# Layer 2's scan of a four-stage network: decay differences moved to ScalarE, trailing parts moved from GpSimd to VectorE

## The chip, the cores and the metric

The kernel runs on one core of a Trainium2 chip. The metric is the device time of one execution in microseconds, the median of several. The engines are named as the profile names them: PE is TensorE (matmuls), DVE is VectorE, ACT is ScalarE, POOL is GpSimd, SP is SyncE, which issues all of this kernel's transfers.

## The reference, cut to what matters

The network has two blocks, each over a sequence of 1024 positions with width 1024. The first block has two layers: one with a gated linear recurrence beside latent attention, and a state space layer, in which the change lies. The second block is a convolution and an attention side by side, an MLP and a gated projection. The state space layer computes, in chunks of 128 positions, with 32 heads of width 64 in 4 groups and a state of 128:

```
def _ssd_scan(x, dt, a_neg, bm, cm):
    ...
    cs = jnp.cumsum(a_dt, axis=2)
    cs_h = jnp.transpose(cs, (0, 1, 3, 4, 2))
    seg = cs_h[..., :, None] - cs_h[..., None, :]
    causal = jnp.tril(jnp.ones((L, L), dtype=bool))
    decay = jnp.where(causal, jnp.exp(jnp.where(causal, seg, 0.0)), 0.0)
    cb = jnp.einsum('bclgn,bcsgn->bcgls', cc, bc)
    y_diag = jnp.einsum('bcghls,bcsghp->bclghp', cb[:, :, :, None] * decay, xf)
    ...
    states = jnp.einsum('bclgn,bclghp->bcghpn', bc, xf * decay_states[..., None])
    ...
    y_off = jnp.einsum('bclgn,bcghpn->bclghp', cc, prev) * jnp.exp(cs)[..., None]
    return (y_diag + y_off).reshape(bsz, seqlen, n_heads, p_dim)
```

The output of the scan gets a skip term, is gated with silu(z), normalized by its group's mean square and projected back to width 1024. All of it is in float32.

## The kernel before

Every float32 product is made of three matmuls on halves: a number is split into a leading part (`hi`, a rounding to the matmul's format, cast on ACT) and a trailing part (`lo`, number minus `hi`, the helper `lo` on line 259), and `mm3` adds hi·hi, hi·lo and lo·hi (lines 188, 192, 193). So each operand of a matmul costs a cast on ACT and a subtraction, on DVE or POOL, whichever the caller names. `weights` (lines 168 to 184) does it for a weight: transfer to `wr`, cast to `wh` (line 179), subtraction to `wl`, in pieces of 128x512 with three buffers of each name; its subtraction goes to POOL unless the caller names an engine.

`phase_b` is the state space layer. It runs 32 steps: 8 units `u` (half a group, 4 heads) times 4 pairs of chunks `cpair`. A step has two halves. `stage1` transposes the inputs on PE, scales them by dt and by the decay to the chunk's end (`Xf`, line 896) and splits them (`Xh` on ACT, `Xl` on POOL). It loads the cumulated logs of the decay, broadcast over partitions, into `L` (128x1024; the tag L has one buffer), subtracts the column `cs_t` of each head and chunk and clips at zero (line 909, 8 instructions of 128x128 on DVE), takes the exponential (line 911, ACT), multiplies by the masked products `cbm` (line 914, DVE, two of 128x512), and splits the result (`Lh` line 916 on ACT, `Ll` on POOL). It also advances the state: a product, then `hs` (lines 932 and 933, DVE), split into `hh` (line 938, ACT) and `hl` (POOL). `stage2` multiplies state and decay matrices into the output: `et` (lines 969 to 986, DVE; line 974 adds the skip term), gates it (`zt`, line 989, DVE), squares it on ACT (line 995) and sums the squares into `acc2` on POOL (lines 997 and 1000). Between the steps, `project` makes the projections for later units (matrices of 128x1024 against all 1024 positions into the PSUM tile `g`): `proj_x` and `proj_bc` are followed by a convolution on DVE (lines 813 and 815), `proj_z` by a gate. At the end of a group `prep_bc` splits and multiplies the next group's B and C (`ch` on ACT, `cl` on POOL). In the last steps `part` starts the output projection, with inputs normalized by `y_act` (line 1072 on DVE, the cast on ACT, the subtraction on POOL). `finish_b` ends it.

The order on each engine is set by a scheduler, which places the instructions of the program by a simulated time line; each engine then works through its own list in order and waits where an instruction's inputs or buffers aren't ready.

Of the kernel before, what the change touches and what calls it, by code (L numbers as in the profile page):

```python
# [11 lines left out]
AF = mybir.ActivationFunctionType  # L12
A = mybir.AluOpType
# [36 lines left out]
class K:  # L50
    def __init__(self, ctx, tc, d):
        self.tc, self.nc, self.d = tc, tc.nc, d
        self.ctx = ctx
        nc = self.nc
        self.cp = ctx.enter_context(tc.tile_pool(name="cp", bufs=1))
        self.wp = ctx.enter_context(tc.tile_pool(name="wp", bufs=3))
        self.dp = ctx.enter_context(tc.tile_pool(name="dp", bufs=1, space=bass.MemoryType.DRAM))
        cp = self.cp
        self.vec = cp.tile([128, NVEC], F32, name="vec")
        self.XH = [cp.tile([128, T], F32R, name=f"XH{k}") for k in range(8)]  # L60
        self.XL = [cp.tile([128, T], F32R, name=f"XL{k}") for k in range(8)]
        self.uid = 0
        self.bp = ctx.enter_context(tc.tile_pool(name="bp", bufs=1, reuse_waits="tile"))
        self.pp = None
        self.it = self.iu = self.ib = 0
        self.side, self.pin = None, False

    @contextmanager
    def phase(self, ns, nh, nd=0, ne=0, nt=3, tmp_p=False):
# [98 lines left out]
    def weights(self, ap, kt, eng=None):  # L168

        nc = self.nc  # L170
        eng = eng or nc.gpsimd
        out = []
        for c in range(0, kt, 4):
            n = min(4, kt - c) * 128
            raw = self.wp.tile([128, HN], F32, tag="wr", bufs=3, name=self.nm("wr"))
            hi = self.wp.tile([128, HN], F32R, tag="wh", bufs=3, name=self.nm("wh"))
            lo = self.wp.tile([128, HN], F32R, tag="wl", bufs=3, name=self.nm("wl"))
            nc.sync.dma_start(raw[:, :n], ap[:, c * 128:c * 128 + n])
            nc.scalar.copy(hi[:, :n], raw[:, :n])  # L179
            self.lo(eng, lo[:, :n], raw[:, :n], hi[:, :n])  # L180
            for j in range(n // 128):
                out.append((hi[:, j * 128:j * 128 + 128], lo[:, j * 128:j * 128 + 128]))
        return out
# [564 lines left out]
    def phase_b(self):  # L748
        nc, v, P, R, cp, d = self.nc, self.v, self.P, self.R, self.cp, self.d
# [9 lines left out]


        first = self.first
        ps = first.pop(0)
        H = slice(0, 32)
        dt, e, cs = P("dt"), P("e"), P("cs")
# [23 lines left out]
        dt_t, w2_t, cs_t = tm[:, 0], tm[:, 1], tm[:, 2]  # L788
# [47 lines left out]
        def prep_bc(g):  # L836
# [10 lines left out]
            nc.scalar.copy(bh, b)  # L847
            self.lo(nc.vector, bl, b, bh)
            nc.scalar.copy(ch, cc)
            self.lo(nc.gpsimd, cl, cc, ch)  # L850
            cbm = P("cbm")
            for n in range(2):
                ps = self.t1()
# [24 lines left out]
        def stage1(u, cpair):  # L878
# [19 lines left out]
                                            fb[:, :, None].to_broadcast([128, 4, 64]), op=A.mult)  # L898
            Xh, Xl = R("Xh"), R("Xl")
            nc.scalar.copy(Xh, Xf)  # L900
            self.lo(nc.gpsimd, Xl, Xf, Xh)

            L = self.tag("L", "L")
            Lv = L.rearrange("p (c h l) -> p c h l", c=2, h=4)
# [1 line left out]
                              csd[c0:c0 + 2, h0:h0 + 4, :].rearrange("c h l -> c (h l)").partition_broadcast(128))  # L906
            for c in range(2):
                for h in range(4):
                    nc.vector.tensor_scalar(Lv[:, c, h, :], Lv[:, c, h, :], cs_t[:, (c0 + c) * 32 + h0 + h:(c0 + c) * 32 + h0 + h + 1],  # L909
                                            0.0, op0=A.subtract, op1=A.min)  # L910
            nc.scalar.activation(L, L, AF.Exp)
            cv = cbm.rearrange("p (c l) -> p c l", c=8)
            for c in range(2):
                nc.vector.tensor_tensor(Lv[:, c], Lv[:, c], cv[:, c0 + c:c0 + c + 1, :].to_broadcast([128, 4, 128]), op=A.mult)
            Lh, Ll = R("Lh"), R("Ll")
            nc.scalar.copy(Lh, L)
            self.lo(nc.gpsimd, Ll, L, Lh)

            prev = []
            pst = self.t1()  # L920
            for c in range(2):
# [14 lines left out]
                hh = self.ph.tile([128, 256], F32R, tag="hh", bufs=4, name=self.nm("hh"))  # L936
                hl = self.ph.tile([128, 256], F32R, tag="hl", bufs=4, name=self.nm("hl"))
                nc.scalar.copy(hh, hn)
                self.lo(nc.gpsimd, hl, hn, hh)
                hst[u] = hn, (hh, hl)  # L940
            stg[u, cpair] = Xh, Xl, Lh, Ll, prev

        def stage2(u, cpair):
# [50 lines left out]
            sq = et  # L994
            nc.scalar.activation(sq, zt, AF.Square)
            if hg == 0:
                nc.gpsimd.tensor_tensor(acc2[g][:, cols], sq[:, 0:256], sq[:, 256:], op=A.add)
            else:
                for p in range(2):
                    nc.gpsimd.tensor_tensor(acc2[g][:, cols], acc2[g][:, cols], sq[:, p * 256:p * 256 + 256], op=A.add)  # L1000
                if cpair % 2:
                    n = cpair // 2
                    s = slice(n * HN, n * HN + HN)
                    ps = self.u1()
                    nc.tensor.matmul(ps, self.ones, acc2[g][:, s], start=True, stop=True)
                    self.rstd_from(acc2[g][:, s], ps, 1.0 / 512, 1e-6)
                    nc.sync.dma_start(self.rsd[g:g + 1, s], acc2[g][0:1, s])
# [56 lines left out]
    def y_act(self, k, hi, lo):  # L1064

        nc, v = self.nc, self.v
        if k % 4 == 0:
            self.rs = self.P("rs")
            nc.sync.dma_start(self.rs, self.rsd[k // 4:k // 4 + 1, :].partition_broadcast(128))
        y = self.P("yl")  # L1070
        nc.sync.dma_start(y, self.yd[k * 128:k * 128 + 128, :])
        nc.vector.scalar_tensor_tensor(y, y, v("snorm", k), self.rs, op0=A.mult, op1=A.mult)
        nc.scalar.copy(hi, y)
        self.lo(nc.gpsimd, lo, y, hi)
        return self.prs(hi, lo)

    def finish_b(self):
        nc, v = self.nc, self.v
        act = [self.y_act(8 + k, self.R("yh"), self.R("yl")) for k in range(4)]
        t = [self.hs(self.P("t")) for m in range(8)]  # L1080
        for n in range(2):
# [844 lines left out]
```

## Time and profile before

| | |
|---|---|
| median of 3 runs | 2819.79 us (2819.03 to 2828.58) |
| profiled execution | 2823.64 us, span 2821.9 us |
| busy in the span: PE, DVE, ACT, POOL | 2639.9, 1998.7, 1366.2, 1091.5 us |
| instructions: PE, DVE, ACT, POOL | 12000, 2740, 2191, 737 |
| steps of the scan (first to last instruction of line 909) | from 576 to 1294 us |

The span is the time from the first to the last instruction of the profiled execution. An engine's busy time is the time in which it has at least one instruction running; instructions of an engine overlap a little at their ends, so a group's count times its mean is a little more than its busy time. A row of groups names the line, the engine, the operation, what is written and read, the shapes and the count; behind the bar stand the busy time, the mean duration and the idle time of the engine just ahead of such instructions.

### The profile page before, as it was taken

What the parts mean: (1) busy time and instruction counts of PE and PEld (TensorE: products, weight loads), DVE (VectorE), ACT (ScalarE), POOL (GpSimd) and SP (SyncE); (2) the same over time, 40 slices, a digit from 0 to 9 for tenths busy, and PEclk for the clock granted to TensorE, in tenths of its full rate; (3) what the DMA queues carried; (4) which work ended last, traced back from release to release, by engine and by line L of the source; (5) the groups of instructions that cost most, each with busy time, mean ns of one, the idle gap of its engine ahead of it and who ended that gap; (6) DMA issues with size and microseconds to landing.
All of it is one profiled execution on the core that took longest, in us unless ns stands there. A gap on an engine that the chain in (4) does not pass through costs nothing. (4 is left out here: it accounts for less than half of the span.)

```text
span 2821.9 us, 34684 instructions
## 1 busy us (share of the span) xinstructions
PE 2639.9 (94%) x12000; PEld 2104.9 (75%) x12000; DVE 1998.7 (71%) x2740; ACT 1366.2 (48%) x2191; POOL 1091.5 (39%) x737
## 2 busy tenths in 40 slices
PE   8999999998888999979899999999899999999997
PEld 6777887776677777758677777767677888887786
DVE  4774766779988899885487212889786666776676
ACT  5554755644443444433265313565665445343465
POOL 2633654445555555575555422656400000000024
PEclk9999999998999989989999999899999999999999
DMA  3444523443334334356533343544464445977324
GB/s 125 159 160 146 141 77 108 148 129 100 117 106 124 111 98 123 108 167 208 167 121 115 94 153 112 155 117 118 136 211 142 146 157 197 340 253 239 111 83 150
DMA packets 214420, 407.15 MB, mean 144 GB/s; under 512 B 22636, under 2 KB 61548, under 8 KB 214244
## 3 DMA queue, kind: packets, MB, share of 16 engines
q1 hardware_dynamic: 214244, 404.93, 44.7%
q8 instruction: 94, 1.54, 0.2%
q14 instruction: 82, 0.67, 0.1%
HBM read 297.35 MB, written 107.50 MB: 143 GB/s over the span
## 5 line engine op out<-in xcount | busy, mean ns | idle before, releaser
L259 POOL TENSOR_TENSOR wl<-wr,wh 128x512 fp32r<-128x512 f32 (+2 forms) x352 | 514.9, 1466 | 1247.3 <-ACT wh L179 1195.4
L188 PE MATMUL g<-XH,wh 128*128 128x512 f32 x1296 | 529.8, 409 | 12.5 <-ACT XH L354 7.5
L192 PE MATMUL g<-XL,wh 128*128 128x512 f32 x1296 | 527.8, 407 | 4.5 <-DVE XL L745 2.3
L193 PE MATMUL g<-XH,wl 128*128 128x512 f32 x1296 | 525.0, 405 | 3.4 <-POOL wl L259 3.4
L179 ACT CAST wh<-wr 128x512 fp32r<-128x512 f32 (+2 forms) x367 | 221.2, 603 | 395.8 <-PE g L192 153.6
L188 PEld LDWEIGHTS g<-XH,wh 128*128 128x128 f32 x1296 | 252.3, 195 | 74.6 <-ACT XH L354 8.2
L192 PEld LDWEIGHTS g<-XL,wh 128*128 128x128 f32 x1296 | 251.6, 194 | 66.4 <-issue 3.5
L193 PEld LDWEIGHTS g<-XH,wl 128*128 128x128 f32 x1296 | 251.7, 194 | 63.0 <-POOL wl L259 4.1
L192 PE MATMUL m<-XL,XH 128*128 128x512 f32 x368 | 145.1, 394 | 6.3 <-DVE XL L259 6.2
L188 PE MATMUL m<-XH,XH 128*128 128x512 f32 x368 | 143.7, 392 | 0.0
L193 PE MATMUL m<-XH,XL 128*128 128x512 f32 x368 | 143.6, 392 | 0.0
L188 PE MATMUL t<-XH,wh 128*128 128x512 f32 (+1 forms) x328 | 129.6, 395 | 4.8 <-ACT wh L179 4.8
L193 PE MATMUL t<-XH,wl 128*128 128x512 f32 (+1 forms) x328 | 130.5, 398 | 2.4 <-POOL wl L259 2.3
L192 PE MATMUL t<-XL,wh 128*128 128x512 f32 (+1 forms) x328 | 129.7, 396 | 0.0
L1281 POOL TENSOR_TENSOR sg<-sg,kp 128x639 f32<-128x639 f32 (+5 forms) x64 | 94.3, 1482 | 67.2 <-DVE kp L1280 60.3
L259 POOL TENSOR_TENSOR Xl<-Xf,Xh 128x1024 fp32r<-128x1024 f32 x32 | 87.0, 2718 | 74.8 <-ACT Xh L900 74.8
L1280 DVE TENSOR_TENSOR_SCAN kp<-kp,zero 128x640 f32<-128x640 f32 (+5 forms) x64 | 106.6, 1680 | 12.2 <-ACT kp L1276 10.8
L1612 ACT CAST XH<-a 128x1024 fp32r<-128x1024 f32 x46 | 48.1, 1049 | 137.5 <-PE m L192 109.9
L909 DVE TENSOR_SCALAR L<-L,tm 128x128 f32<-128x128 f32 x256 | 89.0, 415 | 22.7 <-DMA L<-csd 22.7
L259 DVE TENSOR_TENSOR wl<-wr,wh 128x512 fp32r<-128x512 f32 (+1 forms) x108 | 69.8, 668 | 48.7 <-ACT wh L1528 45.9
L813 DVE SCALAR_TENSOR_TENSOR xc<-xb,hw,xc 128x1021 f32<-128x1021 f32 (+2 forms) x63 | 102.0, 1621 | 3.0 <-ACT xc L810 2.5
L974 DVE SCALAR_TENSOR_TENSOR et<-xc,vec,et 128x256 f32<-128x256 f32 x64 | 102.3, 1637 | 0.4
(583 smaller groups left out, 6779.4 us busy)
## 6 DMA issues: line engine op xcount, KB each, us to landing
a<-w_down SPq DMA_DIRECT2D x64, 512.0 KB, 5.6
b<-hd SPq DMA_DIRECT2D x48, 512.0 KB, 5.7
wr<-wb_in SPq DMA_DIRECT2D x90, 256.0 KB, 3.2
wr<-wc_in SPq DMA_DIRECT2D x72, 256.0 KB, 2.9
L<-csd SPq DMA_DIRECT2D x32, 512.0 KB, 5.0
wr<-w_up SPq DMA_DIRECT2D x28, 512.0 KB, 3.7
wr<-wb_out SPq DMA_DIRECT2D x48, 256.0 KB, 4.5
hd<-t SPq DMA_DIRECT2D x48, 256.0 KB, 2.4
```

The source lines that it names most:

```text
L179: nc.scalar.copy(hi[:, :n], raw[:, :n])
L188: first = nc.tensor.matmul(ps, w[0], a[0], start=start, stop=False, skip_group_check=more)
L192: nc.tensor.matmul(ps, w[0], a[1], start=False, stop=False, skip_group_check=more)
L193: nc.tensor.matmul(ps, w[1], a[0], start=False, stop=stop, skip_group_check=more)
L259: eng.tensor_tensor(out, src, hi.bitcast(F32), op=A.subtract)
L813: nc.vector.scalar_tensor_tensor(xc[:, s:], xb[:, :T - s], hw[:, 24 * k + ci:24 * k + ci + 1], xc[:, s:], op0=A.mult, op1=A.add)
L909: nc.vector.tensor_scalar(Lv[:, c, h, :], Lv[:, c, h, :], cs_t[:, (c0 + c) * 32 + h0 + h:(c0 + c) * 32 + h0 + h + 1], 0.0, op0=A.subtract, ...
L974: nc.vector.scalar_tensor_tensor(ev[:, :, p, :], xt[p][:, cols].rearrange("p (c l) -> p c l", c=2), v("d_skip", 4 * g + 2 * hg + p), ev[:, ...
L1280: nc.vector.tensor_tensor_scan(rv, rv, zero.to_broadcast([128, W]), 1.0, op0=A.mult, op1=A.add)
L1281: nc.gpsimd.tensor_tensor(sg[:, :W - 1], sg[:, :W - 1], kp[:, 1:W], op=A.mult)
L1612: nc.scalar.copy(hi, x)
```

## The change

- The subtraction and the clip on `L` (8 instructions of 128x128 a step on DVE) become 8 activations on ACT, Relu of the column minus `L`; the exponential that follows gets the factor -1. The value is the same.
- The subtractions of `Xl`, `Ll`, `hl` and `cl`, and the sums of squares `acc2`, are put from POOL to DVE.
- In `phase_b` the trailing parts of weights (`wl`) and of `y_act` go to DVE; `finish_b` sets them back to POOL.

By count, 270 instructions go from POOL to DVE: 90 `wl` of 128x512; 32 `Xl`, 32 `Ll`, 4 `cl` and 8 `XL` of `y_act`, each 128x1024; 56 `hl` and 48 sums of 128x256. 256 instructions go from DVE to ACT. PE, SP and the loads of ACT's tables stay the same in number.

```
+        self.weng = tc.nc.gpsimd
...
-        eng = eng or nc.gpsimd
+        eng = eng or self.weng
...
+        self.weng = nc.vector
...
-            self.lo(nc.gpsimd, cl, cc, ch)
+            self.lo(nc.vector, cl, cc, ch)
...
-            self.lo(nc.gpsimd, Xl, Xf, Xh)
+            self.lo(nc.vector, Xl, Xf, Xh)
...
-                    nc.vector.tensor_scalar(Lv[:, c, h, :], Lv[:, c, h, :], cs_t[:, (c0 + c) * 32 + h0 + h:(c0 + c) * 32 + h0 + h + 1],
-                                            0.0, op0=A.subtract, op1=A.min)
-            nc.scalar.activation(L, L, AF.Exp)
+                    nc.scalar.activation(Lv[:, c, h, :], Lv[:, c, h, :], AF.Relu, scale=-1.0,
+                                         bias=cs_t[:, (c0 + c) * 32 + h0 + h:(c0 + c) * 32 + h0 + h + 1])
+            nc.scalar.activation(L, L, AF.Exp, scale=-1.0)
...
-            self.lo(nc.gpsimd, Ll, L, Lh)
+            self.lo(nc.vector, Ll, L, Lh)
...
-                self.lo(nc.gpsimd, hl, hn, hh)
+                self.lo(nc.vector, hl, hn, hh)
...
-                nc.gpsimd.tensor_tensor(acc2[g][:, cols], sq[:, 0:256], sq[:, 256:], op=A.add)
+                nc.vector.tensor_tensor(acc2[g][:, cols], sq[:, 0:256], sq[:, 256:], op=A.add)
...
-                    nc.gpsimd.tensor_tensor(acc2[g][:, cols], acc2[g][:, cols], sq[:, p * 256:p * 256 + 256], op=A.add)
+                    nc.vector.tensor_tensor(acc2[g][:, cols], acc2[g][:, cols], sq[:, p * 256:p * 256 + 256], op=A.add)
...
-        self.lo(nc.gpsimd, lo, y, hi)
+        self.lo(self.weng, lo, y, hi)
...
+        self.weng = nc.gpsimd
```

The scheduler orders the new program anew. One place shows how: the step whose decay matrix is `L_9064`, in the third group of heads. First DVE before, from that matrix's differences to the next step's inputs (in the changed file the lines of the scan are numbered two higher):

```order
L909 TENSOR_SCALAR L_9064<-L_9064,tm 128x128 x5
L932 TENSOR_TENSOR hs_8867<-hs_8858,dec 128x256
L909 TENSOR_SCALAR L_9064<-L_9064,tm 128x128 x3
L872 SCALAR_TENSOR_TENSOR z_8981<-z_8981,g_8932 128x1024
L914 TENSOR_TENSOR L_9064<-L_9064,cbm_8122 128x512 x2
L933 TENSOR_TENSOR hs_8867<-hs_8867,t_8854 128x256
L932 TENSOR_TENSOR hs_9085<-hs_8867,dec 128x256
L896 TENSOR_TENSOR Xf_9055<-t_9050,tm 128x256 x4
```

And DVE of the changed kernel around the same matrix:

```order
L260 TENSOR_TENSOR Xl_9061<-Xf_9055,Xh_9060 128x1024
L260 TENSOR_TENSOR wl_9328<-wr_9326,wh_9327 128x512
L260 TENSOR_TENSOR hl_8861<-hs_8858,hh_8860 128x256
L973 MEMSET et_9109 128x256
L916 TENSOR_TENSOR L_9064<-L_9064,cbm_8122 128x512 x2
L935 TENSOR_TENSOR hs_8867<-hs_8867,t_8854 128x256
L988 TENSOR_TENSOR et_8887<-et_8887,u_8906 64x256 x2
L934 TENSOR_TENSOR hs_9085<-hs_8867,dec 128x256
L991 SCALAR_TENSOR_TENSOR zt_8892<-et_8887,zt_8892 128x256 x2
L260 TENSOR_TENSOR Ll_9078<-L_9064,Lh_9077 128x1024
L935 TENSOR_TENSOR hs_9085<-hs_9085,t_9081 128x256
L260 TENSOR_TENSOR wl_9485<-wr_9483,wh_9484 128x512
```

The eight differences are gone from DVE's list, and the trailing parts stand in it between the other work, six rows (of this merged list) between the product of line 916 and the weight `wl_9485`.

ACT before, around the same matrix (line 911 is the exponential, 916 the cast of the product, 179 the cast of a weight):

```order
L938 CAST hh_8860<-hs_8858 128x256
L911 ACTIVATE L_9064<-L_9064 128x1024
L938 CAST hh_8870<-hs_8867 128x256
L179 CAST wh_9151<-wr_9150 128x512
L179 CAST wh_9321<-wr_9320 128x512
L871 ACTIVATE z_9046<-g_8997 128x1024
L900 CAST Xh_9060<-Xf_9055 128x1024
L916 CAST Lh_9077<-L_9064 128x1024
```

And ACT of the changed kernel (line 911 is now the difference, 913 the exponential, 918 the cast of the product, 180 the cast of a weight):

```order
L911 ACTIVATE L_9064<-L_9064,tm 128x128 x8
L902 CAST Xh_9060<-Xf_9055 128x1024
L180 CAST wh_9327<-wr_9326 128x512
L940 CAST hh_8860<-hs_8858 128x256
L913 ACTIVATE L_9064<-L_9064 128x1024
L918 CAST Lh_9077<-L_9064 128x1024
L180 CAST wh_9484<-wr_9483 128x512
L940 CAST hh_8870<-hs_8867 128x256
```

The eight differences stand in one block, and the casts `Xh_9060`, `wh_9327` and `hh_8860` stand behind that block.

## Rows read from the trace of the kernel before

**Rows 1.** Windows: us from start, length, busy of each engine (count), PEclk, DMA share.

```profile
core 0: us, PE busy (x) PEld busy (x) DVE busy (x) ACT busy (x) POOL busy (x), PEclk, DMA share, GB/s
576.00:1300.00 724.00, 641.36 (x3033) 520.69 (x3032) 625.73 (x966) 303.95 (x391) 408.73 (x255) 0.92 0.40 121
...
750.00:800.00 50.00, 47.54 (x244) 39.11 (x243) 39.46 (x65) 23.99 (x31) 27.29 (x19) 1.00 0.30 96
...
900.00:950.00 50.00, 43.87 (x216) 34.74 (x216) 48.17 (x66) 22.76 (x29) 27.69 (x17) 0.93 0.34 101
```

**Rows 2.** Groups by shape, 576 to 1300 us, DVE: busy us, mean ns, idle before.

```profile
L974 DVE SCALAR_TENSOR_TENSOR et<-xc,vec,et 128x256 f32<-128x256 f32 x60 | 99.5, 1697 | 0.3
L909 DVE TENSOR_SCALAR L<-L,tm 128x128 f32<-128x128 f32 x256 | 89.0, 415 | 22.7 <-DMA L<-csd 22.7
...
L914 DVE TENSOR_TENSOR L<-L,cbm 128x512 f32<-128x512 f32 x64 | 55.4, 906 | 7.1 <-ACT L L911 6.8
...
L896 DVE TENSOR_TENSOR Xf<-t,tm 128x256 f32<-128x256 f32 x128 | 45.4, 413 | 12.6 <-PE t L889 12.5
L813 DVE SCALAR_TENSOR_TENSOR xc<-xb,hw,xc 128x1022 f32<-128x1022 f32 x21 | 41.0, 1953 | 0.1
L932 DVE TENSOR_TENSOR hs<-hs,dec 128x256 f32<-128x256 f32 x48 | 38.5, 803 | 4.7 <-POOL hl L259 2.9
L989 DVE SCALAR_TENSOR_TENSOR zt<-et,zt 128x256 f32<-128x256 f32 x60 | 34.4, 612 | 1.1 <-DMA zt<-zd 0.7
L813 DVE SCALAR_TENSOR_TENSOR xc<-xb,hw,xc 128x1023 f32<-128x1023 f32 x21 | 34.1, 1625 | 0.5
```

**Rows 3.** Four of these lines alone: shortest, median and longest duration in ns.

```profile
L974 DVE SCALAR_TENSOR_TENSOR et<-xc,vec,et x64: 471/1511/2632, 627.7 to 1330.7; 128x256 f32<-128x256 f32 x64
...
L932 DVE TENSOR_TENSOR hs<-hs,dec x48: 410/426/2628, 613.0 to 1289.2; 128x256 f32<-128x256 f32 x48
...
L914 DVE TENSOR_TENSOR L<-L,cbm x64: 675/686/2290, 597.8 to 1295.7; 128x512 f32<-128x512 f32 x64
...
L813 DVE SCALAR_TENSOR_TENSOR xc<-xb,hw,xc x63: 1268/1283/3423, 583.5 to 1201.4; 128x1021 f32<-128x1021 f32 x21, 128x1022 f32<-128x1022 f32 x21, 128x1023 f32<-128x1023 f32 x21
```

**Rows 4.** Timeline of DVE and of POOL near 916 to 924 us: start, duration.

```profile
916.13 0.41 DVE L932 TENSOR_TENSOR hs<-hs,dec 128x256 f32<-128x256 f32 x1
...
921.22 2.63 DVE L932 TENSOR_TENSOR hs<-hs,dec 128x256 f32<-128x256 f32 x1
...
920.89 2.68 POOL L259 TENSOR_TENSOR Xl<-Xf,Xh 128x1024 fp32r<-128x1024 f32 x1 [0.67 <-ACT Xh L900]
```

**Rows 5.** Groups by shape, DVE, 1750 to 2822 us: trailing parts that are already on DVE.

```profile
L259 DVE TENSOR_TENSOR wl<-wr,wh 128x512 fp32r<-128x512 f32 x100 | 66.4, 688 | 48.7 <-ACT wh L1528 45.9 <-ACT wh L179 2.7
L259 DVE TENSOR_TENSOR XL<-a,XH 128x1024 fp32r<-128x1024 f32 x46 | 56.2, 1223 | 20.5 <-ACT XH L1612 20.3
...
L259 DVE TENSOR_TENSOR XL<-t,XL 128x256 fp32r<-128x256 f32 x32 | 12.7, 410 | 1.0 <-ACT XL L576 0.7
```

**Rows 6.** Groups by shape, ACT, whole span: activations of 128x128.

```profile
L1274 ACT ACTIVATE sg<-s 128x128 f32<-128x128 f32 x16 | 4.6, 288 | 6.1 <-PE s L1273 5.9
...
L631 ACT ACTIVATE pn<-g,st 128x128 f32<-128x128 f32 x8 | 3.0, 371 | 0.1
```

**Rows 7.** Waits, 576 to 1300 us: total us, times, longest.

```profile
POOL Xl L259 <- ACT Xh L900: 74.8, 28, 5.2
POOL wl L259 <- ACT wh L179: 71.7, 24, 7.2
POOL hl L259 <- ACT hh L938: 63.5, 25, 5.5
```

**Rows 8.** Timeline of SP and of POOL, one turn of the buffer L.

```profile
982.60 0.38 SPq L905 DMA_DIRECT2D L<-csd  x1
...
1002.98 0.36 SPq L905 DMA_DIRECT2D L<-csd  x1
...
1000.56 2.39 POOL L259 TENSOR_TENSOR Ll<-L,Lh 128x1024 fp32r<-128x1024 f32 x1 [2.70 <-ACT Lh L916]
```

## The prediction

> **What bounds the kernel now.** I read the windows first, to see which engine is full where the change lies. The scan's steps take the stretch from 576 to 1300 us; in these 724 us PE is busy 641.4 us at a granted clock of 0.92, DVE 625.7, POOL 408.7 and ACT 304.0 [rows 1]. Neither PE nor DVE is full on the mean, but they take turns: from 900 to 950 us DVE is busy 48.2 of 50 us and PE 43.9, from 750 to 800 us PE 47.5 at full clock and DVE 39.5 [rows 1]. So in a good part of the stretch DVE is what the others wait for, and its work there is worth cutting.
>
> Second, the groups of DVE by shape, to see whether its instructions take what their sizes ask. They don't. Line 974 works on 128x256 and takes 1.697 us on the mean; line 989, the same operation on the same size, takes 0.612, and line 932, 256 elements too, 0.803 [rows 2]. The shortest of line 974 is 0.471 us, of line 932 0.410, and the longest of both 2.63 [rows 3]. Line 896, which also works on 256 elements but reads PSUM, has a mean of 0.413 [rows 2].
>
> Third, the timeline of DVE beside POOL, to see what stretches them. One product of line 932 takes 0.41 us, the next 2.63: it starts at 921.22, while POOL runs the subtraction `Xl` from 920.89 for 2.68 us, and ends within 0.3 us of it [rows 4]. I take it from this that a DVE instruction with its tensors in SBUF waits until a POOL instruction that was there first has ended. The chip's rows show the stretch, not its cause; that it is POOL is the theory on which the forecast rests.
>
> **The change, part by part.**
>
> *The differences leave DVE.* Their 256 instructions keep DVE busy for 89.0 us, and DVE sat idle 22.7 us ahead of them for the transfer into `L` [rows 2]. Removed: 89.0 us of work. The wait goes along to ACT; whether DVE gets its 22.7 us back depends on whether it then waits for ACT in place of the transfer. Bounds 0 and 22.7. The nearest row is the idle time ahead of line 914, which waits for ACT's exponential now: 6.8 us [rows 2], so DVE mostly finds other work there; but line 914 will then wait for the whole chain from the transfer on. I take half, 11.
>
> *They come to ACT.* The trace has no such activation; the nearest are 128x128 activations of 0.288 us, and of 0.371 with a column from a tile as here [rows 6]. 256 times that is 74 to 95 us more, on an engine that is busy 304 of 724 us [rows 1]; I take 95. With at most 399 us it stays the least busy of the three, so on the path I cost it at nothing. Its cover is that slack; where it fails is that the eight stand in one block on ACT, behind the transfer into `L`, and the casts `Xh`, `wh` and `hh` behind the block wait too. If all 22.7 us of waits for the transfer came back that way on PE's path, that would be the price.
>
> *The trailing parts come to DVE.* Where DVE already does such subtractions, later in the kernel, 100 of 128x512 keep it busy for 66.4 us, 46 of 128x1024 for 56.2 and 32 of 128x256 for 12.7 [rows 5], that is 0.664, 1.222 and 0.397 us each. To come: 90 of the first, 76 of the second, 56 + 48 of the third: 59.8 + 92.9 + 41.3 = 194 us. The sums of squares are priced as subtractions of the same size.
>
> *POOL falls silent, and the stretch with it.* All of POOL's work in this stretch is moved. If the theory holds, DVE's instructions fall to their shortest. By mean and shortest of each line [rows 2, 3]: line 974, 60 x (1.697 - 0.471) = 73.6; line 914, 64 x (0.906 - 0.675) = 14.8; line 813, 21 x (1.953 - 1.268) + 21 x (1.625 - 1.268) = 21.9; line 932, 48 x (0.803 - 0.410) = 18.9; line 989, priced with the 0.471 of line 974, 60 x (0.612 - 0.471) = 8.5. Sum 137.7 us. The bound from below is zero, if the stretch has another cause; I take the whole, since line 896 with its 128 instructions shows no stretch and the timeline shows the pairs.
>
> *Sum for DVE.* 625.7 - 89.0 - 137.7 + 194 = 593 us: 33 us less work, though 270 instructions come and 256 go. With its idle time otherwise unchanged (98 us) the stretch gets 33 us shorter, with half of the wait for `L` 44, which I round to 45.
>
> *Does PE have room?* In the window in which PE runs at full clock it does 244 matmuls in 47.54 us of busy time; 3033 matmuls at that rate are 591 us [rows 1]. In 724 - 45 = 679 us both engines would be busy 87%, beside 86% for DVE now. So the gain isn't cut off by PE, but PE is level with DVE from there on: beyond some 60 us more DVE relief is worth little.
>
> *The buffer of L.* It has one buffer: the transfer of the next step's `L` starts 0.03 us after POOL has ended `Ll`, and two such transfers are 20.4 us apart [rows 8]. Each turn contains `Ll` with 2.39 us [rows 8], which becomes 1.22 on DVE, and one change of engine less (difference and exponential both on ACT). That shortens the turn by at least 1.2 us, 32 times; it isn't added to the sum, since most of the turn is waiting in DVE's list, which the sum has already.
>
> *A rule that speaks against the change.* The rows show min on DVE at 0.415 us each and activations of the size at 0.288 to 0.371 [rows 2, 6], DVE at 86% and ACT at 42% of the stretch. The Trainium skill, page "ScalarE: Activation LUTs", section "Rules for kernel authors", puts relu, max and min on VectorE, not on ScalarE. By that rule the 89.0 us would stay on DVE and its sum would be 682 us in place of 593. I side with the rows: which engine is full decides, and a per-instruction advantage on the full one doesn't count.
>
> Outside of the stretch nothing is changed but the order near its ends. The profiled execution took 2823.64 us, 3.85 more than the median of the runs; the stretch's gain is taken off the median: 2819.8 - 45 = 2774.8 us, say 2775.
>
> **The rivals.**
>
> *Slower: DVE inherits POOL's waits for ACT.* Every trailing part needs the cast of the same tile from ACT just before. POOL sat idle for that 74.8 us ahead of `Xl`, 71.7 ahead of `wl` and 63.5 ahead of `hl`, 210 us in these three rows [rows 7]. On POOL that cost little; on DVE, which works in order, a subtraction whose cast isn't there holds the `et`, `hs` and `Xf` behind it, for which PE waits, and a late `wl` holds a projection. It decides from the point at which the inherited waits eat the 33 us of saved work plus the 11: about a fifth of the 210. If DVE inherits 40%, 84 us, the result is 84 - 45 = 39 us slower, 2859. For it: two lists in order that wait for each other at 270 more places. Against it: the new order of DVE puts other work between a tile's producer and its trailing part (from the product into `L_9064` to `Ll_9078` stand four rows), and ACT is idle more than half of the stretch.
>
> *Slower, and the change doesn't do what it should: the stretch isn't POOL's doing.* Then DVE's sum is 625.7 - 89.0 + 194 = 731 us, more than the stretch now has; with 98 us of idle time the stretch is 829 us, 105 more: 2925. Against it stand rows 4 and the missing stretch of line 896.
>
> *No change: the gain is lost at other places.* Where PE is already full (750 to 800 us [rows 1]) a lighter DVE brings nothing, and the relief of the others is given back by waits of ACT's block and by a fifth of the inherited waits (42 us). The sum is then within a few us of zero, 2815.
>
> *Faster by more.* If DVE's idle share falls to 10% (593 / 0.9 = 659), the gain is 65 us; the floor that PE sets, 591 us at 93%, is 636, a gain of 88 and a time of 2732. What speaks for it: the cut falls into just those windows in which DVE is at 96%, some lines with small stretches aren't in my sum, and PE's clock of 0.92 there can only rise when PE waits less.
>
> **How the numbers follow.** Forecast with its near surroundings (gain of 15 to 70 us): 0.63. Faster by more: 0.11. No change within 0.5%: 0.13. DVE inherits the waits: 0.10. The stretch isn't POOL's: 0.03. A measurement of this kernel can tell about 0.5% (14 us) from no change. So faster by over 0.5% 0.74, within 0.5% 0.13, slower 0.13. The likeliest time is 2775. The range goes from 2732, PE's floor, to 2828, which takes in all of the no-change case and leaves out the two slower ones and a small part of the fast one.
>
> **What will show it.** In the changed kernel's profile: line 974 (now 976) near 0.47 us with its longest well under 1 us, no POOL in the scan's stretch; DVE's busy time in the scan near 593 us and ACT's near 399; the scan's stretch near 679 us; the new trailing parts on DVE at 0.69, 1.22 and 0.41 us each. The step on inherited waits is wrong if the waits of DVE for ACT in the stretch sum to over 44 us; the step on PE's room is wrong if PE's busy time nears the whole stretch. The forecast is wrong if the means of lines 974 and 932 stay stretched with POOL silent, or if stretches appear beside ACT.

## The result

The changed kernel takes 2752.5 us (median of 4 runs, 2749.5 to 2758.0), the kernel before 2823.8 (4 runs): a ratio of 0.9742, 95% interval 0.9715 to 0.9769, or 71 us. Forecast were 2775 us and a range of 2732 to 2828.

The profiled execution took 2749.49 us with a span of 2747.7, against 2821.9 before, 74.2 less. Of these, 2.6 lie ahead of the scan, 60.0 in it (724.0 to 664.0, from the first difference of `L` to shortly behind the last step's product) and 11.6 behind it. The two windows hold nearly the same matmuls (3033 and 3023) but don't end at quite the same work: in the changed kernel the last step's `Xf`, `Xl` and `Ll`, 3.9 us of DVE, come behind 1237.4 us.

The windows of the changed kernel, columns as in [rows 1]: first the scan's stretch, then 50 us in which PE is full, then the worst 50 us.

```profile
573.40:1237.40 664.00, 610.70 (x3023) 506.26 (x3022) 551.61 (x959) 375.15 (x648) 0.00 (x0) 0.95 0.44 132
650.00:700.00 50.00, 50.00 (x268) 42.34 (x267) 47.35 (x88) 28.56 (x50) 0.00 (x0) 1.00 0.47 133
1150.00:1200.00 50.00, 37.90 (x165) 31.25 (x163) 46.76 (x74) 26.33 (x43) 0.00 (x0) 0.76 0.65 213
```

Beside the first row of [rows 1]: POOL went from 408.7 us to none, DVE from 625.7 to 551.6, ACT from 304.0 to 375.2. PE did nearly the same matmuls in 610.7 us in place of 641.4, at a granted clock of 0.95 in place of 0.92, and its idle time fell from 82.6 to 53.3. So the 60 us are half PE's idle time and half PE's pace. PE now runs without a gap in some windows; where it doesn't, as from 1150 to 1200 us, DVE is busy 46.8 of 50 us.

The groups of DVE and ACT by shape in that stretch (busy us, mean ns, idle before); lines 898, 916, 934, 976, 991 are lines 896, 914, 932, 974, 989 of [rows 2], 911 is 909, and the helper's line 259 is now 260.

```profile
L260 DVE TENSOR_TENSOR wl<-wr,wh 128x512 fp32r<-128x512 f32 x80 | 54.8, 685 | 26.4 <-ACT wh L180 26.3
L898 DVE TENSOR_TENSOR Xf<-t,tm 128x256 f32<-128x256 f32 x124 | 44.0, 415 | 4.3 <-PE t L891 4.0
L916 DVE TENSOR_TENSOR L<-L,cbm 128x512 f32<-128x512 f32 x64 | 41.6, 684 | 2.5 <-ACT L L913 2.1
L260 DVE TENSOR_TENSOR Xl<-Xf,Xh 128x1024 fp32r<-128x1024 f32 x31 | 37.9, 1223 | 30.3 <-ACT Xh L902 30.1
L260 DVE TENSOR_TENSOR Ll<-L,Lh 128x1024 fp32r<-128x1024 f32 x31 | 37.8, 1219 | 2.2 <-ACT Lh L918 2.2
L815 DVE SCALAR_TENSOR_TENSOR xc<-xb,hw,xc 128x1022 f32<-128x1022 f32 x21 | 26.8, 1276 | 0.0
L976 DVE SCALAR_TENSOR_TENSOR et<-xc,vec,et 128x256 f32<-128x256 f32 x60 | 26.2, 477 | 0.1
L260 DVE TENSOR_TENSOR hl<-hs,hh 128x256 fp32r<-128x256 f32 x55 | 23.0, 418 | 6.1 <-ACT hh L940 6.0
L991 DVE SCALAR_TENSOR_TENSOR zt<-et,zt 128x256 f32<-128x256 f32 x60 | 22.8, 419 | 0.2
L934 DVE TENSOR_TENSOR hs<-hs,dec 128x256 f32<-128x256 f32 x48 | 20.1, 420 | 0.4
...
L911 ACT ACTIVATE L<-L,tm 128x128 f32<-128x128 f32 x256 | 78.8, 389 | 122.4 <-DMA L<-csd 116.4 <-DVE xc L815 6.0
```

The reader is to see that the stretch is gone from every line that had it: line 976 0.477 us (was 1.697), line 916 0.684 (0.906), line 934 0.420 (0.803), line 991 0.419 (0.612), line 815 1.276 (1.953). Shortest, median and longest of line 976 alone:

```profile
L976 DVE SCALAR_TENSOR_TENSOR et<-xc,vec,et x64: 467/477/485, 624.2 to 1268.4; 128x256 f32<-128x256 f32 x64
```

Line 898, which reads PSUM, is where it was, 0.415 us.

DVE's waits in the stretch (us in total, times, longest):

```profile
DVE Xl L260 <- ACT Xh L902: 30.1, 13, 6.4
DVE wl L260 <- ACT wh L180: 26.3, 12, 4.7
DVE et L973 <- DMA et<-ecd: 7.3, 3, 3.2
DVE hl L260 <- ACT hh L940: 6.0, 5, 2.1
...
DVE Xf L898 <- PE t L891: 4.0, 3, 2.8
```

and the same view of the kernel before:

```profile
DVE hs L935 <- PE t L193: 23.0, 3, 8.6
DVE L L909 <- DMA L<-csd: 22.7, 14, 3.4
DVE Xf L896 <- PE t L889: 12.5, 3, 6.6
DVE t L1040 <- PE g L193: 10.3, 2, 9.0
DVE L L914 <- ACT L L911: 6.8, 8, 1.2
```

By all rows of both answers DVE waits 82 us for ACT (15 before), 12 for PE (47) and 13 for DMA (25). Its idle time is 112 us (98 before): 67 us of new waits for ACT came, and 50 us of other waits went.

### The profile page after: what moved, and what is told of

Its sections match the earlier page's. It is cut to its first block, busy times and chain, and to the rows that moved or that the text cites. A ratio compares the mean times of both kernels' runs of the same rounds, so it can differ in the third digit from the quotient of the medians.

```text
span 2747.7 us, 34501 instructions
## 1 busy us (share of the span) xinstructions
PE 2590.2 (94%) x12000; PEld 2077.2 (76%) x12000; DVE 1933.3 (70%) x2754; ACT 1438.8 (52%) x2447; POOL 655.1 (24%) x467
## 5 line engine op out<-in xcount | busy, mean ns | idle before, releaser
L260 POOL TENSOR_TENSOR wl<-wr,wh 128x512 fp32r<-128x512 f32 (+2 forms) x262 | 371.5, 1422 | 1158.4 <-ACT wh L180 1105.3
L260 DVE TENSOR_TENSOR wl<-wr,wh 128x512 fp32r<-128x512 f32 (+1 forms) x198 | 133.0, 683 | 75.4 <-ACT wh L1531 45.0
L260 POOL TENSOR_TENSOR yl<-yl,yh 128x1024 fp32r<-128x1024 f32 x4 | 9.6, 2400 | 715.0 <-ACT yh L1075 712.3
L911 ACT ACTIVATE L<-L,tm 128x128 f32<-128x128 f32 x256 | 78.8, 389 | 122.4 <-DMA L<-csd 116.4
L577 ACT CAST XL<-t 128x512 fp32r<-128x512 f32 (+2 forms) x192 | 78.4, 426 | 46.1 <-DVE XL L260 21.2
L260 DVE TENSOR_TENSOR XL<-t,XL 128x512 fp32r<-128x512 f32 (+2 forms) x192 | 87.5, 472 | 14.8 <-ACT XL L577 14.0
```

The lines of the kernel that those rows point to most:

```text
L260: eng.tensor_tensor(out, src, hi.bitcast(F32), op=A.subtract)
L577: nc.scalar.copy(th[:, y], ps[:, x])
L911: nc.scalar.activation(Lv[:, c, h, :], Lv[:, c, h, :], AF.Relu, scale=-1.0, bias=cs_t[:, (c0 + c) * 32 + h0 + h:(c0 + c) * 32 + h0 + h + 1])
```

## The experiments

The theories: **first**, a running POOL instruction holds up DVE's instructions on SBUF, and what the change brings is POOL's silence; **second**, changes of engine and slow subtractions stood on the path, and POOL's activity is harmless; **third**, the single buffer of `L` makes a loop of transfer, difference, exponential, product, cast and `Ll` that sets the step, and the change shortens that loop. Every edit lets the scheduler order the whole scan anew; the runs with 16 tiles below show by how much so small an edit can move the time.

**One part alone: the trailing parts and sums.** The changed kernel with the differences back on DVE.

```diff
-                    nc.scalar.activation(Lv[:, c, h, :], Lv[:, c, h, :], AF.Relu, scale=-1.0, bias=cs_t[...])
-            nc.scalar.activation(L, L, AF.Exp, scale=-1.0)
+                    nc.vector.tensor_scalar(Lv[:, c, h, :], Lv[:, c, h, :], cs_t[...], 0.0, op0=A.subtract, op1=A.min)
+            nc.scalar.activation(L, L, AF.Exp)
```

> The changed kernel with the differences of L put back to VectorE; the trailing parts and sums stay there too, so GpSimd is silent in the scan. Theory 1 (a running GpSimd instruction holds up VectorE's instructions on SBUF): the differences come back at 0.277 us each and not at 0.415, line 976 stays at 0.48, VectorE has some 56 us more work than in the changed kernel, and the time is 2780 to 2815 us, between the two. Theory 2 (the gain comes from hand-offs: slow subtractions on the path and one change of engine more or less, GpSimd's activity itself does no harm): one more change of engine a step, 2765 to 2780 us.

Measured: 2777.1 us, 0.9829 (0.9802 to 0.9856) of before. Its scan's windows, and the group of the differences:

```profile
576.30:1251.70 675.40, 619.08 (x3034) 515.90 (x3033) 605.16 (x1223) 308.10 (x394) 0.00 (x0) 0.93 0.42 131
```

```profile
L911 DVE TENSOR_SCALAR L<-L,tm 128x128 f32<-128x128 f32 x256 | 54.8, 280 | 23.3 <-DMA L<-csd 23.2
```

47 of the 71 us come with the trailing parts, and in the profiled executions all of them lie in the scan (724.0 to 675.4 us). Of the other 25, which come with the differences, 11 lie in the scan, 11 behind it and 3 ahead of it, where the differences have no part; the runs with 16 tiles show that a small edit elsewhere can move the time by nearly as much. DVE's busy time fell from 625.7 to 605.2 although 257 instructions were added to it, as the first theory has it; the time itself is a little under that theory's range and fits the second's. The new number is the difference: 0.280 us on DVE when POOL is silent, against 0.415 in [rows 2]. A third of what looked like its price was stretch too.

DVE's waits in this scan show a second thing:

```profile
DVE L L911 <- DMA L<-csd: 23.2, 13, 5.0
...
DVE wl L260 <- ACT wh L180: 7.6, 6, 3.0
...
DVE Xl L260 <- ACT Xh L902: 3.9, 4, 1.1
```

By all rows DVE waits 20 us for ACT here, 15 before and 82 in the changed kernel. So the trailing parts alone brought few waits for their casts; most came with the differences, which stand on ACT in one block ahead of casts. One place in the changed kernel, DVE first, then ACT (start, duration):

```profile
1231.90 0.69 DVE L260 TENSOR_TENSOR wl<-wr,wh 128x512 fp32r<-128x512 f32 x1 [4.47 <-ACT wh L180]
...
1228.91 2.45 ACT L911 ACTIVATE L<-L,tm 128x128 f32<-128x128 f32 x8 [9.23 <-DMA L<-csd]
1231.26 0.60 ACT L180 CAST wh<-wr 128x512 fp32r<-128x512 f32 x1
```

The cast `wh` stands behind a block that waited 9.23 us for its transfer, and DVE waited 4.47 us for that cast. DVE's idle time in the scan is 98 us before, 70 here and 112 in the changed kernel: of the 54 us of work that the differences take off DVE, 42 come back as idle time.

**The other part alone: the differences on ACT**, with POOL as before.

```diff
-                    nc.vector.tensor_scalar(Lv[:, c, h, :], Lv[:, c, h, :], cs_t[...], 0.0, op0=A.subtract, op1=A.min)
-            nc.scalar.activation(L, L, AF.Exp)
+                    nc.scalar.activation(Lv[:, c, h, :], Lv[:, c, h, :], AF.Relu, scale=-1.0, bias=cs_t[...])
+            nc.scalar.activation(L, L, AF.Exp, scale=-1.0)
```

> The kernel before with only the differences of L on ScalarE; GpSimd keeps its subtractions. Theory 1: GpSimd still holds up VectorE, line 974 stays above 1.2 us on the mean, VectorE loses its 89 us of differences but other instructions collide in their place; 2770 to 2805 us, so less than the whole gain. Theory 2: the hop is gone, the slow subtractions stay; 2795 to 2815 us, line 974 unchanged.

Measured: 2827.0 us, 0.9996 (0.9977 to 1.0016): nothing. Both expectations missed. Windows, three groups and the longest waits of DVE in the scan:

```profile
575.10:1293.40 718.30, 636.29 (x3033) 517.82 (x3032) 551.05 (x709) 379.58 (x651) 409.15 (x255) 0.92 0.41 122
```

```profile
L974 DVE SCALAR_TENSOR_TENSOR et<-xc,vec,et 128x256 f32<-128x256 f32 x60 | 70.3, 1206 | 0.6
L914 DVE TENSOR_TENSOR L<-L,cbm 128x512 f32<-128x512 f32 x64 | 70.2, 1136 | 56.3 <-ACT L L911 49.7 <-issue 4.2 <-POOL hl L259 2.0
L989 DVE SCALAR_TENSOR_TENSOR zt<-et,zt 128x256 f32<-128x256 f32 x60 | 51.7, 902 | 1.2 <-DMA zt<-zd 0.9
```

```profile
DVE L L914 <- ACT L L911: 49.7, 15, 6.1
DVE Xf L896 <- PE t L889: 37.2, 7, 7.8
DVE et L971 <- ACT L L911: 13.1, 2, 6.5
```

This is the most telling pair of rows in the study. DVE is busy 551 us here and 552 in the changed kernel, yet the scan takes 718 us here and 664 there. A sum of an engine's busy time doesn't set the time by itself: of the 75 us that DVE was relieved of, 69 became idle time (98 to 167 us), the largest part of it ahead of line 914, which now waits 49.7 us for ACT's exponential behind the block of differences and is then stretched as well (1.136 us, 0.906 before). Together with the run before: the differences bring at most 25 us on a silent POOL (2777.1 to 2752.5, 11 of them in the scan) and nothing beside a busy one.

**POOL's activity by itself.** The changed kernel with three subtractions on POOL in each step, in place in `Xf`, which no one reads any more; no result is changed.

```diff
             self.lo(nc.vector, Xl, Xf, Xh)
+            for i in range(3):
+                self.lo(nc.gpsimd, Xf, Xf, Xh)
```

> The changed kernel, and in each of the 32 steps GpSimd subtracts Xh from Xf three times in place after Xl is made (128x1024; Xf has no reader after that), some 240 us of GpSimd for which nobody waits but the reuse of that buffer. Theory 1: line 976 rises from 0.48 to about 1 us on the mean with its longest near 2.5, VectorE is busy 50 to 100 us more, and the time is 2790 to 2840 us. Theory 2: the time is that of the changed kernel within 8 us (2745 to 2761) and line 976 stays at 0.48.

Measured: 2916.2 us, 1.0316 (1.0287 to 1.0345), 164 over the changed kernel. Windows of the scan, then groups of DVE (behind line 903 its line numbers are 2 higher than the changed kernel's) and of POOL:

```profile
573.70:1379.40 805.70, 662.04 (x3010) 539.49 (x3009) 724.31 (x958) 376.72 (x648) 260.20 (x93) 0.87 0.35 108
```

```profile
L918 DVE TENSOR_TENSOR L<-L,cbm 128x512 f32<-128x512 f32 x64 | 87.1, 1394 | 0.3
...
L993 DVE SCALAR_TENSOR_TENSOR zt<-et,zt 128x256 f32<-128x256 f32 x60 | 50.7, 882 | 0.2
L898 DVE TENSOR_TENSOR Xf<-t,tm 128x256 f32<-128x256 f32 x124 | 43.9, 413 | 4.8 <-PE t L891 4.4
...
L937 DVE TENSOR_TENSOR hs<-hs,t 128x256 f32<-128x256 f32 x47 | 19.3, 411 | 1.6 <-PE t L194 1.3
...
L260 POOL TENSOR_TENSOR Xf<-Xf,Xh 128x1024 f32<-128x1024 f32 x93 | 260.2, 2798 | 547.8 <-DVE Xl L260 423.5 <-issue 61.4 <-PE g L193 58.0
```

and the timeline near 914 us (start, duration), POOL first:

```profile
913.60 7.56 POOL L260 TENSOR_TENSOR Xf<-Xf,Xh 128x1024 f32<-128x1024 f32 x3 [14.12 <-DVE Xl L260]
...
913.77 5.16 DVE L978 SCALAR_TENSOR_TENSOR et<-xc,vec,et 128x256 f32<-128x256 f32 x2
918.86 3.38 DVE L260 TENSOR_TENSOR Ll<-L,Lh 128x1024 fp32r<-128x1024 f32 x1
922.16 0.68 DVE L260 TENSOR_TENSOR wl<-wr,wh 128x512 fp32r<-128x512 f32 x1
```

POOL's three run one after the other, 2.52 us each. Two of line 978, 0.48 us each when undisturbed, end about when POOL's first and second end; `Ll` (1.22 us undisturbed) ends at 922.24, which is 1.08 us after POOL's third. In the scan DVE's busy time rose by 724.3 - 551.6 = 173 us for 260 us of POOL, 0.66 us for each. Most lines with all their tensors in SBUF are stretched (of the larger ones not `Xl`, behind which POOL's three start); those that read PSUM (898, 937) aren't. No wait in this trace's scan names POOL as the engine waited for, so the price isn't that of a buffer that came free late. The first theory is shown, the second falls. Its sizes were missed: 50 to 100 us more of DVE and at most 2840 us were expected, and of line 978 a mean of about 1 us, where it is 0.689 with a longest of 2.62.

The Trainium skill, page "GPSIMD Engine Reference", section "8. Key points", says that GpSimd shares its SBUF interfaces with VectorE and contends with VectorE's instructions that have two SBUF inputs or run in a two-port mode. The rows agree as far as they go: lines 918 and 993 have two inputs in SBUF, lines 898 and 937 take one from PSUM. The difference, with one tensor input, went from 0.280 to 0.415 us beside POOL; which mode it runs in no row says.

**Weights back on POOL.** The changed kernel without the line that sets the weights' engine, so that `wl` and the trailing parts of `yl` are POOL's again.

```diff
-        self.weng = nc.vector
```

> The changed kernel with the trailing parts of the weights and of y_act back on GpSimd (90 of 128x512, 8 of 128x1024). Theory 1: VectorE loses some 55 us of work and is held up again by about 125 us of GpSimd, a third of what it was, some 40 us; the two nearly cancel, 2740 to 2775 us, and line 976 is at 0.6 to 1.0 us. Theory 2: no waits of VectorE for the casts of weights (26 us less), 2725 to 2750 us, line 976 at 0.48.

Measured: 2772.2 us, 0.9817 (0.9786 to 0.9849), 20 over the changed kernel. The scan's windows:

```profile
574.20:1242.80 668.60, 608.82 (x3016) 496.05 (x3015) 566.51 (x875) 375.29 (x647) 147.19 (x87) 0.96 0.42 131
```

Taking some 64 us of subtractions off DVE made DVE busier, 566.5 us for 551.6. The scan is 5 us longer, the rest lies elsewhere; 20 us is little more than a new order can bring (below), so that it didn't help is what this run shows, not that it hurts. The time is in the first theory's range and over the second's; the mean of line 976 (here 975), 0.544 us, lies between the two. The Trainium skill, "Perfetto Trace Analysis", section "Optimizing Scalar/DVE Operations", says that offloading between GpSimd and DVE might not help; here it agrees.

**`Ll` alone on POOL**, and **`Ll` alone on DVE**: first in the changed kernel

```diff
-            self.lo(nc.vector, Ll, L, Lh)
+            self.lo(nc.gpsimd, Ll, L, Lh)
```

> The changed kernel with only Ll back on GpSimd (32 of 128x1024). Theory 3: each turn of the loop of L is at least 1.35 us longer (2.57 for 1.22), times 32, 2785 to 2810 us. Theory 1: VectorE loses 38 us of work and is held up by 82 us of GpSimd, for which e3 showed 0.66 us of VectorE for each us, 54; 2755 to 2780 us.

Measured: 2786.1 us, 0.9863 (0.9834 to 0.9891), 34 over the changed kernel: just inside the third theory's range and 6 over the first's. POOL's 31 subtractions take 95.1 us in place of 82, and DVE, though rid of 37.8, is busy 567.2: 53 us of stretch, 0.56 for each us of POOL. How much of the 34 us is this stretch and how much the slower `Ll` itself, this run doesn't tell.

Its trace shows that the wait goes the other way too (POOL first, then DVE):

```profile
1003.49 4.26 POOL L260 TENSOR_TENSOR Ll<-L,Lh 128x1024 fp32r<-128x1024 f32 x1 [15.46 <-ACT Lh L918]
...
1003.66 1.22 DVE L817 SCALAR_TENSOR_TENSOR xc<-xb,xc 128x1024 f32<-128x1024 f32 x1
1004.79 0.69 DVE L260 TENSOR_TENSOR wl<-wr,wh 128x512 fp32r<-128x512 f32 x1
1005.39 0.41 DVE L935 TENSOR_TENSOR hs<-hs,t 128x256 f32<-128x256 f32 x1
1005.73 3.09 DVE L815 SCALAR_TENSOR_TENSOR xc<-xb,hw,xc 128x1021 f32<-128x1021 f32 x1
```

The shortest `Ll` on POOL takes 2.37 us, this one 4.26. While it stood, DVE ran line 817 and `wl`, with both inputs in SBUF, at their undisturbed lengths; counted back from its end, POOL's work began near 1005.4, when DVE came to line 935, which reads PSUM. The line behind that took 3.09 us in place of 1.28 and ended 1.07 after POOL. So here POOL waited for DVE's instructions first, and then DVE for POOL's.

Then the reverse, in the kernel that had only the differences on ACT.

```diff
-            self.lo(nc.gpsimd, Ll, L, Lh)
+            self.lo(nc.vector, Ll, L, Lh)
```

> The kernel before with the differences on ScalarE and Ll on VectorE, the other subtractions on GpSimd. Theory 3: one turn of the loop gets 1.35 us shorter against the run with the differences alone (2827 us), 2775 to 2800 us. Theory 1: 39 us more work for VectorE and a fifth less of GpSimd, 2815 to 2840 us.

Measured: 2835.9 us, 1.003 (1.0012 to 1.0049): in the first theory's range, far from the third's. This version has the short loop of `L`, on ACT and DVE, and gains nothing while POOL works elsewhere.

**Two buffers of `L`**, which opens the loop; a tile of the shared pool has to go for the room (16 in place of 17). In the kernel before, then in the changed one; and as a control 16 tiles with one buffer (the second edit alone), in both.

```diff
-TAGS = dict(Z=1, L=1, S=4)
+TAGS = dict(Z=1, L=2, S=4)
...
-            with self.phase(17, 4, 0, 4, 2):
+            with self.phase(16, 4, 0, 4, 2):
```

> The kernel before with two buffers for L and one less (16 for 17) of the shared 128x1024 tiles, which pays for it. Theory 3 (the single buffer of L makes a loop of load, difference, exponential, product, cast and subtraction, and that loop sets the step): the load goes under the rest, 5 to 6 us a step leave the loop; 2700 to 2770 us. Theory 1 alone (VectorE held up by GpSimd sets the step): VectorE's work is unchanged, 2805 to 2830 us.

> The changed kernel with two buffers for L and 16 shared tiles. Theory 3: the loop is still what sets the step, 2690 to 2735 us. Theory 1: TensorE and VectorE share the bound now, 2740 to 2760 us.

> The same control for the kernel before: if the missing tile made it 34 us slower, about 2860; if not, 2815 to 2835.

> Control for the changed kernel with two buffers of L: 16 shared tiles in place of 17 and still one buffer of L. If the missing tile is what made that version 20 us slower, about 2770 here; if the second buffer itself did it (or the other order that it gives), 2745 to 2760, as the changed kernel.

Measured: 

| | 17 tiles, one L | 16 tiles, one L | 16 tiles, two L |
|---|---|---|---|
| before | 2823.8 | 2837.6, 1.0045 (1.0027 to 1.0063) | 2861.0, 1.0126 (1.0097 to 1.0154) |
| changed | 2752.5 | 2771.0, 0.9814 (0.9782 to 0.9845) | 2773.0, 0.9821 (0.9787 to 0.9855) |

The two runs with two buffers lie above the ranges of both theories. The edit did open the loop: with one buffer no transfer into `L` starts before the `Ll` of the step before has ended, with two all 31 start 7 to 53 us ahead of that end. At equal tiles the second buffer brings nothing in the changed kernel (2 us slower) and costs 23 in the one before. So the third theory falls as what sets the step. The control shows a second thing: one shared tile less, at the same instructions on every engine, costs 14 and 18 us. It gives the scheduler less room and so another order; an edit as small as that moves this kernel by that much, and differences under 20 us between versions here prove nothing about a mechanism.

**POOL silent elsewhere too.** The changed kernel with the weights kept on DVE behind the scan, to the end; then also in layer 1 and in the norms, so that POOL keeps 138 instructions of the 737 that it had before.

```diff
     def finish_b(self):
...
-        self.weng = nc.gpsimd
+        self.weng = nc.vector
...
-                self.lo(nc.gpsimd, lo, y, hi)
+                self.lo(nc.vector, lo, y, hi)
```

and for the second, besides

```diff
-        self.weng = tc.nc.gpsimd
+        self.weng = tc.nc.vector
...
-            self.lo(eng or (nc.vector if m % 2 else nc.gpsimd), self.XL[m][:, s], x, self.XH[m][:, s])
+            self.lo(eng or nc.vector, self.XL[m][:, s], x, self.XH[m][:, s])
```

with the same step at five more calls, most of them in layer 1.

> The changed kernel, with the trailing parts of the weights and of yl kept on DVE after the scan too, to the end of the kernel (176 subtractions, some 120 us at the 0.685 us measured in the scan, in place of 246 us on POOL). PE is busy 1445.6 of the 1510.3 us after the scan there, so little is to be had: PE's waits for POOL there are some 11 us, its waits for DVE some 35. If POOL's activity costs DVE 0.66 us per us (as in the run with added POOL work), DVE's busy time after the scan stays near its 1002 us (+120 - up to 160) and the time falls by 5 to 25: 2728 to 2748. If hand-offs between engines were what mattered, DVE's busy time there rises to 1100 and the time is 2750 to 2775.

> As the run before it, and also layer 1's trailing parts on DVE, with the alternating ones of the norms: POOL keeps only its 134 products (lines 634, 1284, 1775). If a silent POOL is what frees DVE, another 5 to 20 us: 2715 to 2745, with the DVE lines that read SBUF in layer 1 near their shortest. If hand-offs were what mattered: 2755 to 2790, since DVE takes over 94 more waits for ACT ahead of wl.

Measured: 2749.8 us (2741.6 to 2758.5), 0.9741 (0.971 to 0.9772), the same as the changed kernel; and 2759.3, 0.9778 (0.9752 to 0.9804), 7 over it. The first lies between its two ranges, the second in the one that goes with hand-offs; neither is further from the changed kernel than a new order can bring. The windows behind the scan, changed kernel first:

```profile
1237.40:2747.70 1510.30, 1445.56 (x6359) 1134.45 (x6357) 1002.33 (x1289) 738.17 (x1232) 395.16 (x278) 0.98 0.49 161
```

```profile
1241.20:2756.70 1515.50, 1460.85 (x6359) 1148.47 (x6357) 1038.73 (x1469) 740.00 (x1232) 143.98 (x98) 0.97 0.48 160
```

180 more instructions on DVE, 125 us at the scan's durations (176 x 0.685 and 4 x 1.22), and its busy time rose by only 36: the stretch goes with POOL here as well, some 80 us by the durations of the other lines. But PE is busy 96% of this stretch, and nothing came of it. The mechanism is the same, the gain isn't; my expectation of 5 to 25 us took PE's few waits for DVE there (35 us) as if the stretch caused them.

## Why the prediction was right, and where its sizes were off

**What bounds the kernel.** Right: the scan's stretch held 60 of the 74 us, and PE and DVE took turns there. For the rest of the kernel the prediction has nothing; 14 us came there, which is the size that a new order alone can bring.

**The stretch is POOL's.** Right, and shown by the added POOL work. In size 149 us by means and counts of the two traces, forecast 138: lines 817 and 1074, which weren't in the sum, had 4 and 7 us of it.

**The differences leave DVE: 89.0 us.** As a busy time they were 54.8 us once POOL was silent; the other 34 were stretch and went with POOL's silence, not with the move. And most of the 54.8 came back as idle time, so that the move is worth 11 us in the scan and at most 25 in all. The prediction added the 89 to the other terms as if the part stood alone, and alone it gave nothing.

**The wait for the transfer into `L`: half of 22.7.** Line 916 now waits only 2.1 us for the exponential, so the one row that the prediction looked at came out well. But ACT idles 116 us for the transfer, and the wait came to DVE at other lines: ahead of `Xl` and `wl` DVE waits 56.4 us for their casts, 11.5 with the differences on DVE.

**The differences on ACT: nothing on the path.** The work was priced at 0.288 to 0.371 us each and measured 0.389, 78.8 us in all, inside the 74 to 95; ACT is busy 375 us, forecast at most 399. The path was mis-sized. The prediction names how its slack can fail, by the casts behind the block, with a price of up to 22.7 us, and counts nothing: DVE's waits for ACT rose by 62 us (20 to 82) and its idle time by 42 with this part. One difference takes 0.280 us on DVE and 0.389 on ACT, and the run with the differences on DVE was 25 us slower all the same. The Trainium skill ("ScalarE: Activation LUTs", "Rules for kernel authors") puts relu, max and min on VectorE; for one instruction these rows agree with it. For the kernel the 25 us speak against it, so far as they go beyond what a new order brings.

**The trailing parts on DVE.** Priced at 0.664, 1.222 and 0.397 us, measured 0.685, 1.22 and 0.418. In the stretch they come to 186 us, forecast 194, since 80 of the 90 weights fall into it.

**The sum.** Forecast -33 us of DVE work, measured 625.7 to 551.6, -74. The larger stretch explains 11 of the 41 between, the trailing parts 8. The other 22 are overlapping ends: the sum puts busy times, in which an overlap counts once, beside means times counts, in which it doesn't. DVE's durations add up to 58 us more than its busy time before and to 82 more with the trailing parts on it, so these cost less than their durations.

**Where luck came in.** Without the differences the prediction's terms give DVE 56 us more work (194 - 138), and the differences then take 89 off and 11 of waiting. Measured, the trailing parts alone gave DVE 20 us less work and 28 less idle time and made the scan 49 us shorter, and the differences then made it 11 shorter. So the total of 45 came near the measured 60 of the scan because one part was taken for far too little and the other for far too much. That POOL's silence pays was forecast and is shown; that it would pay without the differences doesn't follow from the prediction's sum.

**DVE's idle time.** Forecast to fall by 11, it rose by 14. By the prediction's own sign, over 44 us of DVE's waits for ACT, its step on inherited waits is wrong: there are 82. But they aren't the waits that the rival "DVE inherits POOL's waits for ACT" has in mind. With all trailing parts on DVE and the differences still there, DVE waits 20 us for ACT, 15 before; of POOL's 210 us ahead of `Xl`, `wl` and `hl` it took over 11.5. Those three rows are 62.4 in the changed kernel: most of it came with the block of differences on ACT. It didn't undo the gain, since DVE's waits for PE fell by 35 us and those for transfers by 12. Forecast from its parts the stretch was 724 - 33 - 11 = 680; with the measured sizes it is 724 - 74 + 14 = 664.

**PE's room.** Right in kind: PE is full in some windows now, at 610.7 us against a floor of 591. Part of the gain is its clock, 0.92 to 0.95, which only the fast rival counted.

**The rivals.** The measured 71 us lie at the edge between the forecast's own range (15 to 70) and that of "faster by more" (65 to 88); but the reason given for the latter, DVE's idle share falling to 10%, didn't occur (112 of 664 us, 17%). That the stretch isn't POOL's is refuted. Not settled: how much of the trailing parts' 47 us is DVE's relief and how much their shorter durations (`Ll` 1.22 us in place of 2.57). Nor what holds the scan with the differences alone at 718 us; DVE's busy sum doesn't, a second buffer of `L` wasn't tried there, and whether it is the stretched instructions in the chain from the transfer to `Ll` was not measured apart.

## What to carry to other kernels

When equal instructions of DVE differ by whole microseconds, look in the timeline at what POOL runs at that moment; work "offloaded" to POOL is partly paid by DVE, here 0.56 to 0.66 us for each us of POOL, so a subtraction moved back can make DVE less busy. Such a relief is worth time only where DVE is late: the same silence brought 47 us in the scan and nothing where PE is busy 96%. Before work goes to an emptier engine, look at what stands behind it in that engine's list: a block that waits for a transfer holds up the casts behind it, and through them the engine that was to be relieved. Price an edit in the company of the others, keep to one measure (mean times count, or busy time) in a sum, and find out by a nearly neutral edit how much a new order alone moves the time before reading a mechanism from a small difference.

## What the runs showed of the hardware that was not expected

- The wait is for the end of the POOL instruction, each time anew: DVE's 0.48 us instruction took 2.6 us behind one of 2.52, the next one again. Lines that take an input from PSUM kept 0.411 to 0.415 us in the same steps.
- POOL waits for DVE as well: `Ll` on POOL took 4.26 us at 1003.49 for a shortest of 2.37, while DVE ran two-input instructions on SBUF at their undisturbed lengths. The subtraction of 128x1024 that took 2.52 us in the three at 913.60 took 2.80 on the mean of 93.
- The differences, which looked regular at a mean of 0.415 us, were stretched too: 0.280 with POOL silent.
- The granted clock was lower where PE idled more: 0.95 in the changed kernel's scan (PE idle 53 of 664 us), 0.92 before (83 of 724), 0.87 with the added POOL work (144 of 806). It isn't strict: with the weights back on POOL it was 0.96 (60 of 669).
